# Expert slots dealt in strides, and three kept output tiles, in a float32 block with a 32-expert mixture

## The chip, the cores and the metric

The kernel runs on one core of one Trainium2 chip, as one launch. The metric is the device time of one execution in microseconds (us), as the median of the runs shown.

## What is computed

Two blocks run one after the other on 1024 tokens of 1024 float32 values. The first has a gated linear attention, a pooled branch and, at its end, a mixture of experts; the second has a short convolution and three dilated window attentions. The change is in the mixture of experts of the first block. Cut to what matters, it is

```
g_p, g_idx = top_k(softmax(h @ w_rg + b_rg), 1)            # one of 4 groups
e_top, e_idx = top_k(logits of that group's 8 experts, 2)  # two of its 8 experts
gate = g_p * softmax(e_top)
y[assignment] = gate * (silu(x @ w_gate[e]) * (x @ w_up[e])) @ w_down[e]
out[token] += y of its two assignments
```

So 1024 tokens make 2048 assignments to 32 experts of width 256. Each expert's three weight matrices are 1 MB each, 3 MB together.

## The kernel before, in words

All products are made in three passes: both factors are split into a rounded high part and a rest (`split`, lines 131 to 137: ScalarE makes the high part, VectorE the rest), and `mm3` (lines 166 to 169) adds three matmuls. So every weight tile that arrives costs ScalarE and VectorE an instruction each before TensorE can use it.

**Places and slots.** The router gives each assignment a place within its expert (`posk`, line 688): 0, 1, 2 and so on. Each expert has `CAP` = 96 slots, one for each partition of a tile of 96 rows. For each token tile, lines 690 to 695 compare a constant row 0, 1, ..., 127 (`iota_s`, lines 399 to 400) with the places and get a 0/1 matrix `sel`; matmuls with it (lines 718 to 724) put, for every expert, the token's number and the assignment's number into the slot that the place names (`row_idx`, `row_place`, lines 739 to 747). A slot that no assignment fills gets a number out of bounds. Assignments from place 96 on would be done by a loop behind the experts (lines 1239 to 1322), whose number of turns is computed on the chip.

**One expert.** `fetch` (line 1095) gathers an expert's rows from memory by an indirect DMA on GpSimd's queue, partition p getting the row that slot p names (lines 1074 to 1077); an out-of-bounds slot moves nothing. `turn_rows` transposes them, `into` makes the gate and up products, `turn_act` transposes the activation, `down` (lines 1140 to 1157) makes the output product, scales the rows on ScalarE into a tile `yt` (lines 1148 to 1150), and `put_expert` scatters those rows to memory by another indirect DMA on GpSimd's queue (lines 1081 to 1091). The last expert's rows are not read back from memory: `place_last` (lines 1165 to 1172) makes 0/1 rows `picks` with which TensorE adds them to the first 512 tokens (lines 1174 to 1184).

**The order of the work.** The loop over the 32 experts is written out in lines 1217 to 1235. In the turn of expert e, the rows of e + 3 are fetched, the weights of e + 5 are loaded, expert e's gate product is made, the rows of e + 1 are turned, then e - 1's activation is turned, e's up product is made, and e - 1's output product. Engines run in order; a scheduler at build time puts each engine's instructions into a sequence, ordered mostly as they are written.

**Buffers.** `load_expert` (lines 272 to 292) makes six loads of 512 KB for an expert, two each of gate, up and down. A load waits for the fifth load before it (`QD` = 5). The loads go round 27 buffers: 4 of tag "wr", 4 of tag "wb" and 19 of tag "blk". The tag "blk" has 26 buffers of 4 KB a partition in all (`NBLK`), which are shared by everything that asks for one with `blk(...)`: during the experts four hold gathered rows (`xg`), and the others go to loads and to the `yt` tiles as they come free. Line 1148 asks for a new `yt` for each expert.

```
        yt = blk("yt", (P, D))
        for n in range(2):
            A.activation(yt[:CAP, halves[n]], yps[n], AF.Copy, scale=row_wgt[:CAP, e:e + 1])
        if e < NE - 1:
            put_expert(e, yt)
```

Of the kernel before, what the change touches and what calls it, by code (L numbers as in the profile page):

```python
# [12 lines left out]
F32 = mybir.dt.float32  # L13
# [4 lines left out]
OP = mybir.AluOpType  # L18
AX = mybir.AxisListType

P = 128
T = 1024
D = 1024
# [4 lines left out]
NE = 32  # L28
NOB = 21
CAP = 96  # L30
# [35 lines left out]
def first_then_second_block(ctx: ExitStack, tc: tile.TileContext, a: dict, out: bass.AP):  # L66
    nc = tc.nc
    V, A, G, PE, SY = nc.vector, nc.scalar, nc.gpsimd, nc.tensor, nc.sync
    late = Later()

    C = ctx.enter_context(tc.tile_pool(name="const", bufs=1))
# [13 lines left out]
    def blk(name, shape=(P, 2, 512), dtype=F32):  # L85
        return B.tile(list(shape), dtype, name=name, tag="blk", bufs=NBLK)

    def psum(shape, name="ps"):
        t = PS.tile([P, 512], F32, name=name, tag="ps")
        n = int(np.prod(shape[1:]))  # L90
        v = t[: shape[0], :n]
        if len(shape) == 3:
            v = v.rearrange("p (a b) -> p a b", a=shape[1])
        elif len(shape) == 4:
            v = v.rearrange("p (a b c) -> p a b c", a=shape[1], b=shape[2])
        return v
# [299 lines left out]
    V.tensor_scalar(tri16[:64, :P], tri16[:64, :P], -1.0 / 16, None, op0=OP.add)  # L396
    V.memset(tri16[:64, P:], 1.0 / 16)
    V.memset(tri16[64:, P:], 0.0)
    iota_s = C.tile([P, P], F32, name="iota_s")
    G.iota(iota_s, pattern=[[1, P]], base=0, channel_multiplier=0, allow_small_or_imprecise_dtypes=True)  # L400
    rank8 = C.tile([P, 8], F32, name="rank8")
    V.tensor_scalar(rank8, iota_s[:, :8], -1.0, 8.0, op0=OP.mult, op1=OP.add)
    pcol = C.tile([P, 1], F32, name="pcol")
    G.iota(pcol, pattern=[[1, 1]], base=0, channel_multiplier=1, allow_small_or_imprecise_dtypes=True)
    cnt = W.tile([P, 4, 16], F32, name="cnt")
    for g, wd in enumerate((2, 4, 8, 16)):
        V.tensor_scalar(cnt[:, g, :], iota_s[:, :16], 1.0, float(wd), op0=OP.add, op1=OP.min)
    V.reciprocal(cnt, cnt)


# [25 lines left out]
    for base in (0, -36):  # L436
        G.affine_select(out=fold, in_=fold, compare_op=OP.not_equal, fill=1.0, base=base, pattern=[[-1, 36]],
                        channel_multiplier=1)
# [63 lines left out]
    at = {}  # L502
# [134 lines left out]
    def small(name, shape, dtype=F32):  # L637
        return R.tile([P] + list(shape), dtype, name=name, tag=name, bufs=1)
# [36 lines left out]
    def places(hf, val, gp, e1, e2):  # L675
        ts = slice(4 * hf, 4 * hf + 4)
        pp = psum((P, 4, NE))
        for i in range(4):
            t = 4 * hf + i
            for tt in range(t):  # L680
                PE.matmul(pp[:, i, :], onesb, asg[:, tt, :], start=tt == 0, stop=False)
            PE.matmul(pp[:, i, :], before, asg[:, t, :], start=t == 0, stop=True)
        ex = small("ex", (4,))
        V.tensor_sub(ex, e2, e1)
        A.activation(ex, ex, AF.Exp)
        pr = small("pr", (4, 2, NE))
        V.tensor_mul(pr, oh[:, ts], pp[:, :, None, :].to_broadcast([P, 4, 2, NE]))
        V.tensor_reduce(posk[:, ts, :], pr, axis=AX.X, op=OP.add)
        sels = []
        for i in range(2):  # L690
            sel = R.tile([P, 4, P], BF16, name="sel", tag="sel", bufs=2)
            pos = posk[:, 4 * hf + 2 * i:4 * hf + 2 * i + 2, :].rearrange("p t k -> p (t k)")
            V.tensor_tensor(sel, iota_s[:, None, :].to_broadcast([P, 4, P]), pos[:, :, None].to_broadcast([P, 4, P]),
                            op=OP.is_equal)
            sels.append(sel)

        def weigh():
            den = small("den", (4,))
            V.tensor_scalar(den, ex, 1.0, None, op0=OP.add)
            V.reciprocal(den, den)  # L700
            w2 = small("w2", (4, 2))
            V.tensor_mul(w2[:, :, 0], gp, den)
            V.tensor_mul(w2[:, :, 1], w2[:, :, 0], ex)
            rest = small("rest", (4, 2))
            V.tensor_copy(wgt[:, 0, ts, :], w2)
            V.tensor_sub(rest, w2, wgt[:, 0, ts, :])
            V.tensor_copy(wgt[:, 1, ts, :], rest)
            V.tensor_sub(wgt[:, 2, ts, :], rest, wgt[:, 1, ts, :])
            V.tensor_mul(val.rearrange("p t k v e -> p (t k) v e")[:, :, 3:, :],
                         oh[:, ts].rearrange("p t k e -> p (t k) e")[:, :, None, :].to_broadcast([P, 8, 3, NE]),  # L710
                         wgt[:, :, ts, :].rearrange("p j t k -> p (t k) j")[:, :, :, None].to_broadcast([P, 8, 3, NE]))

        late.at(1 if hf else PLACES, lambda: slots(hf, val, sels, weigh))

    def slots(hf, val, sels, weigh):
        if hf == 0:
            weigh()
        for v0 in (0, 3):
            ps = psum((P, 3, NE))
            for i in range(4):  # L720
                for k in range(2):
                    PE.matmul(ps.rearrange("p a b -> p (a b)"), sels[i // 2][:, 2 * (i % 2) + k, :],
                              val[:, i, k, v0:v0 + 3].rearrange("p a b -> p (a b)"),
                              start=i == 0 and k == 0, stop=i == 3 and k == 1)
            if hf == 0:
                sums.append(R.tile([P, 3, NE], F32, name=f"sums{v0}"))
                V.tensor_copy(sums[-1], ps)
            else:
                sv = sums[v0 // 3]
                if v0 == 0:  # L730
                    V.tensor_add(sv, sv, ps)
                    sums.append(extra[0].tile([P, NE], I32, name="row_place"))
                    with tc.issue_after(row_places(row_idx, sums[2], sv, NE, R).ins):
                        weigh()
                    continue
                V.tensor_add(sv, sv, ps)
                row_weights(row_wgt, sv[:, 0, :], sv[:, 1, :], sv[:, 2, :])
# [331 lines left out]
    wg, wu, wd = w_experts  # L1069
# [20 lines left out]
            tc.declare_no_dep(ins, other, reason="rows of their own")  # L1090
        puts.append(ins)

    xT, gu, act, aT, yp = {}, {}, {}, {}, {}

    def fetch(e):
        return gather_rows(xg[e % (FA + 1)], row_idx[:, e:e + 1], CAP)
# [13 lines left out]
    def expert_tiles(k, n):  # L1110
        n_split[0] += 1
        if n_split[0] % (3 + NX) < 3:
            return split_tiles(k, n)
        return [E.tile([P, k, n], F32R, name="ehl", tag="ehl", bufs=2 * NX) for _ in range(2)]
# [25 lines left out]
    def down(e):  # L1140
        ah, al = aT[e]
        yps = [psum((CAP, 512)) for _ in range(2)]
        for k in range(2):
            hi, lo = expert_tiles(2, 512)
            split(hi, lo, raws[e][4 + k])
            for n in range(2):
                mm3(yps[n], (ah[:, k, :], al[:, k, :]), (hi[:, n, :], lo[:, n, :]), k == 0, k == 1)
        yt = blk("yt", (P, D))
        for n in range(2):
            A.activation(yt[:CAP, halves[n]], yps[n], AF.Copy, scale=row_wgt[:CAP, e:e + 1])  # L1150
        if e < NE - 1:
            put_expert(e, yt)
        else:
            yhl = [blk("yhl", (P, D), F32R) for _ in range(2)]
            for n in range(2):
                split(yhl[0][:CAP, halves[n]], yhl[1][:CAP, halves[n]], yt[:CAP, halves[n]])
            last_y.extend([yt] + yhl)
# [5 lines left out]
    picks = []  # L1163

    def place_last():
        at = E.tile([P, 5], F32, name="last_at")
        picks.append(blk("picks", (P, 512), F32R))
        V.tensor_copy(last_place, row_place[:, NE - 1:NE])
        V.tensor_copy(at[:, 4:], row_idx[:, NE - 1:NE])
        for i in range(4):  # L1170
            V.tensor_scalar(at[:, i:i + 1], at[:, 4:], float(-P * i), None, op0=OP.add)
            V.tensor_scalar(picks[0][:, i * P:(i + 1) * P], iota_s, at[:, i:i + 1], None, op0=OP.is_equal)

    def add_last(c):
        for y in yc2[c]:
# [13 lines left out]
    load_expert(4, after=fetched[0])  # L1189
    turn_rows(0)  # L1190

    iota_e = iota_s[:, :NE]
    cnt_e = E.tile([P, NE], F32, name="cnt_e")
    more = E.tile([P, NE], F32, name="more")
    scan = [E.tile([P, NE], F32, name=f"scan{i}") for i in range(2)]
# [21 lines left out]
    for e in range(NE):  # L1217
# [14 lines left out]
        if e:  # L1232
            down(e - 1)
    turn_act(NE - 1)
    down(NE - 1)

    xc2, turn_part2 = load_cols(x_acc, "x2c")
    end_reg = nc.values_load(n_more[0:1, 0:1], min_val=0, max_val=NOB)
    with tc.For_i(0, end_reg, 1):
        mine = E.tile([P, NE], F32, name="mine")  # L1240
        left = E.tile([P, NE], F32, name="left")
# [2 lines left out]
        V.tensor_scalar(mine, mine, number, None, op0=OP.is_le)  # L1244
        V.tensor_mul(mine, mine, left)
        part = E.tile([P, 2], F32, name="part")
        V.tensor_mul(left, mine, iota_e)
        V.tensor_reduce(part[:, 0:1], left, axis=AX.X, op=OP.add)
        V.tensor_sub(left, more, ends)
        V.tensor_scalar(left, left, number, None, op0=OP.add)  # L1250
# [7 lines left out]
        pos = E.tile([P, NT, 2], F32, name="pos")  # L1258
# [14 lines left out]
        for t in range(NT):  # L1273
            for k in range(2):
                sel = E.tile([P, P], BF16, name="lsel", tag="lsel", bufs=2)
                V.tensor_scalar(sel, iota_s, pos[:, t, k:k + 1], None, op0=OP.is_equal)
                PE.matmul(sp, sel, rv[:, t, k, :], start=t == 0 and k == 0, stop=t == NT - 1 and k == 1)
        li = E.tile([P, 1], I32, name="li")
        lw = E.tile([P, 1], F32, name="lw")
# [14 lines left out]
        for i, w in enumerate((wg, wu)):  # L1294
            src = w[bass.ds(e_reg, 1)].rearrange("o (p k) n -> p (o k) n", p=P)
            for q in range(2):
                wt = blk("lwt", (P, 4, 256))
                SY.dma_start(wt, src[:, 4 * q:4 * q + 4, :])
                for kk in range(4):
                    k = 4 * q + kk  # L1300
# [23 lines left out]
    for c in range(4):  # L1324
        yc2.append([])
        for k in range(2):
            yt = blk("y2c", (P, 4, 256))
# [586 lines left out]
```

## Time and profile before

| | us |
|---|---|
| median of three runs | 1574.97 (1574.22 to 1577.56) |
| the profiled execution | 1581.15 |
| its span, first to last instruction | 1579.4 |
| TensorE (PE) busy in it | 1513.8 (96%) |
| VectorE (DVE) busy | 1041.1 (66%) |
| ScalarE (ACT) busy | 803.6 (51%) |
| GpSimd (POOL) busy | 153.7 (10%) |

The profile is one execution. Times in it count from its first instruction. In rows of instructions, "out<-in" names the tiles written and read, and what stands in brackets at the end is how long the engine had been idle before, and what ended that. PE is TensorE's matmuls, PEld its weight loads, SPq the queue on which SyncE issues DMAs. The granted clock is 1.00 at 2.4 GHz and 0.50 at 1.2 GHz.

### The profile page before, as it was taken

Reading aid. Unit: us, or ns where it says so; the run is one execution under the profiler, and the core shown is the slowest. Engines: PE = TensorE matmul, PEld = TensorE weight load, DVE = VectorE, ACT = ScalarE, POOL = GpSimd, SP = SyncE. Lnnn points to the kernel's source line nnn. Section 1 sums busy time; section 2 is a strip of 40 time slices with the busy share of each in tenths; the row PEclk is TensorE's granted clock in tenths of the full one; section 3 lists DMA queues with packets and bytes.
Section 4 is the critical chain, followed back from the end, with each engine's and each line's share of the span. In section 5 each row is a group of like instructions: output and inputs, shape, how many; then the busy total and the mean of one; then the engine's idle time right before and its main releaser. Section 6 shows DMA issues by size and latency. Waiting matters only on the chain. (4 is left out here: it accounts for less than half of the span.)

```text
span 1579.4 us, 24063 instructions
## 1 busy us (share of the span) xinstructions
PE 1513.8 (96%) x8694; PEld 1253.4 (79%) x8694; DVE 1041.1 (66%) x2309; ACT 803.6 (51%) x1656; POOL 153.7 (10%) x180
## 2 busy tenths in 40 slices
PE   8999999999999995999989996999999999999999
PEld 6888888887888884998979885788878888777777
DVE  6586444777744346897978887765975645677762
ACT  5534322453433232787879784522543324877750
POOL 2000000000000002231212110200100000022211
PEclk9999999999999997999999997999999999999999
DMA  6223334556422367999999998436534222355545
GB/s 212 81 58 119 95 108 172 185 180 188 120 81 81 120 241 270 301 315 349 340 324 353 308 350 262 146 127 231 186 91 133 92 82 73 95 130 151 143 143 173
DMA packets 175445, 284.59 MB, mean 180 GB/s; under 512 B 33968, under 2 KB 117307, under 8 KB 175196
## 3 DMA queue, kind: packets, MB, share of 16 engines
q1 hardware_dynamic: 161484, 244.19, 47.9%
q0 software_dynamic: 13824, 38.84, 7.3%
q8 instruction: 69, 1.13, 0.3%
q14 instruction: 52, 0.43, 0.1%
q10 hardware_dynamic: 16, 0.00, 0.0%
HBM read 252.30 MB, written 43.78 MB: 187 GB/s over the span
## 5 line engine op out<-in xcount | busy, mean ns | idle before, releaser
L133 ACT CAST wh<-wr 128x512 fp32r<-128x512 f32 (+1 forms) x248 | 170.5, 716 | 344.8 <-PE ps L168 190.5
L133 DVE TENSOR_TENSOR wl<-wr,wh 128x512 fp32r<-128x512 f32 (+1 forms) x248 | 196.0, 808 | 157.0 <-ACT wh L133 149.5
L133 DVE TENSOR_TENSOR wl<-ew,wh 128x1024 fp32r<-128x1024 f32 x144 | 172.5, 1220 | 30.9 <-ACT wh L133 27.6
L167 PE MATMUL ps<-h,wh 128*128 128x512 f32 x448 | 176.0, 393 | 0.0
L169 PE MATMUL ps<-h,wl 128*128 128x512 f32 x448 | 174.6, 390 | 0.0
L168 PE MATMUL ps<-h,wh 128*128 128x512 f32 x448 | 174.5, 390 | 0.0
L133 ACT CAST wh<-ew 128x1024 fp32r<-128x1024 f32 x144 | 149.3, 1049 | 34.2 <-PE ps L169 26.8
L167 PE MATMUL ps<-g,wh 128*128 128x512 f32 x320 | 125.9, 394 | 0.0
L168 PE MATMUL ps<-g,wh 128*128 128x512 f32 x320 | 125.2, 392 | 0.0
L169 PE MATMUL ps<-g,wl 128*128 128x512 f32 x320 | 124.9, 391 | 0.0
L167 PE MATMUL ps<-wh,xh 128*96 128x256 f32 x384 | 109.5, 285 | 0.4 <-ACT act L1128 0.4
L168 PE MATMUL ps<-wl,xh 128*96 128x256 f32 x384 | 108.8, 283 | 0.5 <-DVE wl L133 0.5
L169 PE MATMUL ps<-wh,xh 128*96 128x256 f32 x384 | 108.6, 283 | 0.0
L169 PEld LDWEIGHTS ps<-h,wl 128*128 128x128 f32 x448 | 84.1, 188 | 17.8
L167 PEld LDWEIGHTS ps<-h,wh 128*128 128x128 f32 x448 | 84.1, 188 | 17.6
L168 PEld LDWEIGHTS ps<-h,wh 128*128 128x128 f32 x448 | 84.2, 188 | 17.1
L167 PE MATMUL ps<-wh,g 128*128 128x512 f32 x192 | 76.4, 398 | 0.0
L169 PE MATMUL ps<-wh,g 128*128 128x512 f32 x192 | 75.0, 391 | 0.0
L168 PE MATMUL ps<-wl,g 128*128 128x512 f32 x192 | 74.8, 390 | 0.0
L167 PEld LDWEIGHTS ps<-g,wh 128*128 128x128 f32 x320 | 60.4, 189 | 13.0 <-issue 0.6
L168 PEld LDWEIGHTS ps<-g,wh 128*128 128x128 f32 x320 | 60.4, 189 | 12.5 <-DVE g L136 0.2
L169 PEld LDWEIGHTS ps<-g,wl 128*128 128x128 f32 x320 | 60.4, 189 | 12.5
(467 smaller groups left out, 3520.4 us busy)
## 6 DMA issues: line engine op xcount, KB each, us to landing
wr<-in_w_in_dram SPq DMA_DIRECT2D x128, 512.0 KB
ew<-in_w_exp_down_dram SPq DMA_DIRECT2D x64, 512.0 KB
ew<-in_w_exp_gate_dram SPq DMA_DIRECT2D x64, 512.0 KB
ew<-in_w_exp_up_dram SPq DMA_DIRECT2D x64, 512.0 KB
wr<-in_w_out_dram SPq DMA_DIRECT2D x24, 512.0 KB
xs<-xb_rows POOLq DMA_DIRECT2D x28, 256.0 KB
x<-in_x_dram SPq DMA_DIRECT2D x12, 512.0 KB
zb<-sw_d SPq DMA_DIRECT2D x24, 256.0 KB
```

The lines of the kernel that those rows point to most:

```text
L133: both = A.copy(hi, src), V.tensor_sub(lo, src, hi.bitcast(F32))
L167: PE.matmul(ps, lhs[0], rhs[0], start=start, stop=False)
L168: PE.matmul(ps, lhs[0], rhs[1], start=False, stop=False)
L169: PE.matmul(ps, lhs[1], rhs[0], start=False, stop=stop)
```

## The change

Four things change, all about which slot a place gets, and about `yt`.

A constant `slot_s` takes the place of `iota_s`. Its columns 0 to 95 hold, in column 6a + b, the number a + 16b; columns 96 to 127 hold their own number. Where slots are found (lines 693 and 1276), the places are compared with it, so place a + 16b goes to slot 6a + b. `seq` is the same memory read in the order in which it holds 0, 1, ..., 95; where the plain row was wanted (`rank8`, `cnt`, the overflow loop and `picks`) it is read through `seq`, in steps of six columns, and `picks` is written in two pieces. `yt` is no longer asked for anew: the first three experts make a tile each, and expert e uses the tile e mod 3.

```diff
-    iota_s = C.tile([P, P], F32, name="iota_s")
-    G.iota(iota_s, pattern=[[1, P]], base=0, channel_multiplier=0, allow_small_or_imprecise_dtypes=True)
+    slot_s = C.tile([P, P], F32, name="slot_s")
+    G.iota(slot_s[:, :CAP].rearrange("p (a b) -> p a b", a=16), pattern=[[1, 16], [16, CAP // 16]], base=0, channel_multiplier=0,
+           allow_small_or_imprecise_dtypes=True)
+    G.iota(slot_s[:, CAP:], pattern=[[1, P - CAP]], base=CAP, channel_multiplier=0, allow_small_or_imprecise_dtypes=True)
+    seq = slot_s[:, :CAP].rearrange("p (a b) -> p b a", a=16)
...
-    V.tensor_scalar(rank8, iota_s[:, :8], -1.0, 8.0, op0=OP.mult, op1=OP.add)
+    V.tensor_scalar(rank8, seq[:, 0, :8], -1.0, 8.0, op0=OP.mult, op1=OP.add)
...
-        V.tensor_scalar(cnt[:, g, :], iota_s[:, :16], 1.0, float(wd), op0=OP.add, op1=OP.min)
+        V.tensor_scalar(cnt[:, g, :], seq[:, 0, :], 1.0, float(wd), op0=OP.add, op1=OP.min)
...
-            V.tensor_tensor(sel, iota_s[:, None, :].to_broadcast([P, 4, P]), pos[:, :, None].to_broadcast([P, 4, P]),
+            V.tensor_tensor(sel, slot_s[:, None, :].to_broadcast([P, 4, P]), pos[:, :, None].to_broadcast([P, 4, P]),
...
-    xT, gu, act, aT, yp = {}, {}, {}, {}, {}
+    xT, gu, act, aT, yts = {}, {}, {}, {}, []
...
-        yt = blk("yt", (P, D))
+        if len(yts) < 3:
+            yts.append(blk("yt", (P, D)))
+        yt = yts[e % 3]
...
-            V.tensor_scalar(picks[0][:, i * P:(i + 1) * P], iota_s, at[:, i:i + 1], None, op0=OP.is_equal)
+            row = picks[0][:, i * P:(i + 1) * P]
+            V.tensor_scalar(row[:, :CAP].rearrange("p (b a) -> p b a", a=16), seq, at[:, i:i + 1], None, op0=OP.is_equal)
+            V.tensor_scalar(row[:, CAP:], slot_s[:, CAP:], at[:, i:i + 1], None, op0=OP.is_equal)
...
-        V.tensor_mul(left, mine, iota_e)
+        V.tensor_mul(left.rearrange("p (b a) -> p b a", a=16), mine.rearrange("p (b a) -> p b a", a=16), seq[:, :NE // 16, :])
...
-                V.tensor_scalar(sel, iota_s, pos[:, t, k:k + 1], None, op0=OP.is_equal)
+                V.tensor_scalar(sel, slot_s, pos[:, t, k:k + 1], None, op0=OP.is_equal)
```

## Rows read from the trace of the kernel before

**Rows 1.** The page's slices: busy tenths in 40 equal parts of the span.
```profile
PE   8999999999999995999989996999999999999999
...
DMA  6223334556422367999999998436534222355545
```
**Rows 2.** Windows: us, busy us (instructions) by engine, clock, DMA share, GB/s.
```profile
core 0: us, PE busy (x) PEld busy (x) DVE busy (x) ACT busy (x) POOL busy (x), PEclk, DMA share, GB/s
660.00:940.00 280.00, 267.14 (x1930) 240.96 (x1929) 238.16 (x303) 232.53 (x330) 61.34 (x53) 0.98 0.96 335
...
920.00:940.00 20.00, 19.63 (x144) 17.48 (x144) 18.45 (x27) 18.10 (x27) 2.92 (x3) 1.00 1.01 397
```
**Rows 3.** Timeline of GpSimd: start us, us, instruction; gathers (L1075) and puts (L1082).
```profile
721.93 0.96 POOL L1075 DMA_INDIRECT xg<-h_rows,row_idx  x1 [3.16 <-PE ps L1136]
...
736.97 0.96 POOL L1075 DMA_INDIRECT xg<-h_rows,row_idx  x1 [8.51 <-PE ps L1136]
...
793.98 0.96 POOL L1075 DMA_INDIRECT xg<-h_rows,row_idx  x1 [3.20 <-PE ps L1136]
...
808.73 1.02 POOL L1082 DMA_INDIRECT y_rows<-yt,row_place  x1 [4.30 <-ACT yt L1150]
812.95 0.96 POOL L1075 DMA_INDIRECT xg<-h_rows,row_idx  x1 [3.21 <-PE ps L1136]
...
829.09 0.96 POOL L1075 DMA_INDIRECT xg<-h_rows,row_idx  x1 [8.49 <-PE ps L1136]
```
**Rows 4.** Timeline of ScalarE at three places of the expert stage.
```profile
725.99 1.26 ACT L1150 ACTIVATE yt<-ps,row_wgt 96x512 f32<-96x512 f32 x2 [4.77 <-DMA y_rows<-yt,row_place]
...
818.13 1.26 ACT L1150 ACTIVATE yt<-ps,row_wgt 96x512 f32<-96x512 f32 x2 [5.90 <-DMA y_rows<-yt,row_place]
...
894.82 0.38 ACT L1128 ACTIVATE act<-ps 96x256 f32<-96x256 f32 x1
...
908.53 0.37 ACT L1128 ACTIVATE act<-ps 96x256 f32<-96x256 f32 x1
...
916.08 1.05 ACT L133 CAST wh<-ew 128x1024 fp32r<-128x1024 f32 x1 [3.18 <-DMA ew<-in_w_exp_gate_dram]
...
921.02 0.38 ACT L1128 ACTIVATE act<-ps 96x256 f32<-96x256 f32 x1
```
**Rows 5.** Timeline of TensorE: its three longest idle times within the experts.
```profile
728.26 0.47 PE L167 MATMUL ps<-wh,ah 128*96 128x512 f32 x1 [3.58 <-ACT ah L133]
...
820.40 0.47 PE L167 MATMUL ps<-ehl,ah 128*96 128x512 f32 x1 [4.67 <-ACT ah L133]
...
908.96 0.36 PE L167 MATMUL ps<-ehl,xh 128*96 128x256 f32 x1 [3.60 <-ACT act L1128]
```
**Rows 6.** Window just behind the first of them (columns as in group 2).
```profile
728.80:732.10 3.30, 3.30 (x9) 2.07 (x9) 3.05 (x5) 3.29 (x4) 0.00 (x0) 0.50 1.04 363
```
**Rows 7.** Waits of SyncE's queue, 560 to 980 us: us in total, times, longest.
```profile
SPq L286 <- DMA ew<-in_w_exp_gate_dram: 94.7, 47, 8.6
...
SPq L286 <- DVE wl L133: 6.5, 19, 0.7
```
**Rows 8.** Line 286, 600 to 960 us: issue ns min/median/max, first and last start.
```profile
L286 SPq DMA_DIRECT2D ew<-in_w_exp_down_dram x60: 327/328/1153, 607.8 to 939.2; - x60
```
**Rows 9.** Timeline of SyncE's queue.
```profile
705.92 0.59 SPq L286 DMA_DIRECT2D ew<-in_w_exp_gate_dram  x1
706.56 1.15 SPq L286 DMA_DIRECT2D ew<-in_w_exp_down_dram  x1
715.30 0.93 SPq L286 DMA_DIRECT2D ew<-in_w_exp_gate_dram  x2
...
721.34 2.40 SPq L286 DMA_DIRECT2D ew<-in_w_exp_gate_dram  x2
```
**Rows 10.** Timelines of GpSimd and TensorE at the start of the experts.
```profile
623.28 1.04 POOL L1075 DMA_INDIRECT xg<-h_rows,row_idx  x1 [8.81 <-DVE last_at L1171]
...
631.45 0.88 PE L1104 MATMUL ps<-ident,xg 96*128 96x96 f32 x4 [5.64 <-DMA xg<-h_rows,row_idx]
```
**Rows 11.** Line 1172: ns min/median/max, first and last start.
```profile
L1172 DVE TENSOR_SCALAR picks<-iota_s,last_at x4: 281/281/282, 918.3 to 918.9; 128x128 fp32r<-128x128 f32 x4
```

More of the change, by code (lines that the diff above doesn't have):

```diff
@@ L1190, in first_then_second_block @@
     turn_rows(0)
-    iota_e = iota_s[:, :NE]
     cnt_e = E.tile([P, NE], F32, name="cnt_e")
```

## The prediction

> **What bounds the kernel now.** I read the page's strip of slices first [rows 1]. TensorE is at nine tenths or more in nearly every slice, so the change can only return time where TensorE stands idle. The DMA strip is at nine in the eight slices from 632 to 948 us, which are the experts. There the windows [rows 2] show, from 660 to 940 us, TensorE busy 267.1 of 280 us, DMA engines 96% busy and 335 GB/s moved. So the stage has two near-limits: TensorE's own work, and the stream of expert weights with the row gathers and puts beside it.
>
> The pace of TensorE without a wait is read from the gathers, one per expert [rows 3]: from 793.98 to 812.95 us are two steps, so 9.48 us an expert. The next step in the same rows takes 16.14 us (812.95 to 829.09), and that from 721.93 to 736.97 takes 15.04 us. A third long stretch is in ScalarE's rows [rows 4]: the activations of three experts in a row start at 894.82, 908.53 and 921.02 us, 26.20 us where two steps are 18.96. The three cost 5.56, 6.66 and 7.24 us: **19.5 us** in all. TensorE's idle time in them is 3.58, 4.67 and 3.60 us [rows 5]; most of the rest is the slower clock after each, granted 0.50 in the 3.3 us that the window shows (the 1.2 GHz level) [rows 6].
>
> What ends them differs. In the first two, ScalarE waits 4.77 and 5.90 us at line 1150 to write `yt`, until a put has landed [rows 4]. Before the longer wait, which ends at 818.13, the last put was issued at 808.73 [rows 3], 9.4 us earlier: the new output tile had got the buffer of the expert just before it. ScalarE's next work, the splits that TensorE needs, stands behind that wait. In the third, ScalarE waits for expert weights, 3.18 us at its longest [rows 4].
>
> The weight stream itself is paced by its own landings: SP's queue waits 94.7 us on earlier loads of gate weights alone, against 6.5 us on VectorE's splits freeing a buffer [rows 7]. Loads of down weights, two of an expert's six, are issued 60 times from 607.8 to 939.2 us [rows 8]: 59 steps of 5.62 us, 11.23 us an expert. TensorE eats one in 9.48. The 27 buffers of the ring are a lead of 4.5 experts, 42.7 us of work; at 1.75 us lost per expert it is gone after 24 experts. The third stall comes at expert 27. That fits a stream that is too slow, not an accident.
>
> **The change, part by part.** *Three kept output tiles.* `yt` of expert e now takes the tile of expert e-3, whose put was issued three experts, some 28 us, before; the longest wait seen for a put ended 9.4 us after its issue. Both put stalls go: 5.56 + 6.66 = 12.2 us. But the loads were on their way during those stalls and did not stop, so this alone moves nothing at the end: TensorE would reach the third stall 12.2 us sooner and wait there 12.2 us longer. The gain is real only if the stream gets faster: to have no third stall, its weights (the cast that waits for them starts at 916.08 [rows 4], 308 us after the 607.8 of [rows 8]) must come 19.5 us sooner, which is 6.3%.
>
> *Places in strides.* Slot column c = 6a + b now holds place a + 16b. An expert has 2048/32 = 64 rows on average for its 96 slots; the others hold an index out of bounds and move nothing. If the 96 slots are cut into 16 runs of six, one for each DMA engine, the first engine had 6 + 6 rows of 4 KB per expert from gather and put, the last ones none, and the mean is 4 + 4. A weight load puts 8 rows of 4 KB on each engine, so six loads are 48. The fullest engine goes from 60 rows to 56 per expert, **6.7%** less, and a load lands when its last engine is done. That is an estimate from the code; no row tells which engine moved which slot. It just covers the 6.3%. Bounds: 0, if the rows were spread already, to 6.7%.
>
> *Order of the loads.* The 26 shared buffers less four for gathered rows are 22, for which loads and `yt` compete; a load with no buffer is overtaken by one of another tag. SP's rows show it [rows 9]: a single gate load stands ahead of a down load at 706.56, where in turn it would be two gate, two up, two down, and from that one's end, 707.71, to 715.30 nothing is issued for 7.6 us; a pair in turn, at 721.34, takes 2.4 us. Now 26 - 4 - 3 = 19 are left, exactly the loads' share, so I expect the regular order. Bounds of this: 0 to what the best window shows, 397 GB/s at 920 to 940 us against 335 [rows 2]; at 397 an expert's six loads and 128 rows (3.67 MB) take 9.24 us, under TensorE's 9.48. I take the upper side, since both rates stand in this stage: stream fast enough, third stall gone, **7.2 us**. Next in line is VectorE, with 238 of then some 260 us [rows 2].
>
> *The first gather.* TensorE waits 5.64 us for it; issued at 623.28, it lets TensorE start at 631.45, 8.17 us [rows 10]. Expert rows on the fullest engine fall by a third, so the bounds are 0 and 2.7 us; much of the time is before any data moves, I take **1.0 us**.
>
> *What is added.* `picks`: four compares of 128 columns at 281 ns [rows 11] become four of 96, strided, and four of 32. An instruction of 32 columns takes at most those 281 ns, so this adds up to 1.1 us; were the strided ones twice as long as well, 2.2 us. VectorE is 238 of 280 us busy there [rows 2], and no instruction waits on `picks` before the end of the experts: 0, with 2.2 us if that cover is gone. One more iota on GpSimd at the very start, before any weights have come, costs 0. `sel`, `rank8` and `cnt` keep shape and count. The loop for overflowing experts never ran (its lines have no row), so its lines cost 0.
>
> Sum: 12.2 + 7.2 + 1.0 = 20.4 us. The profiled execution took 1581.15 us (span 1579.4), 6.2 above the median of 1574.97; 1581.15 - 20.4 = 1560.7, and from the median, 1554.5.
>
> **The rivals.** *The stream gains half of what is needed* (3.15% of 308 us, 9.7 us): the third stall stays at 19.5 - 9.7 = 9.8 us. Gain 9.7 + 1 = 10.7: 1564; with less or more, 1562 to 1569. For it: 60 to 56 only just covers the need, and batches may remain.
>
> *The stream stays as it is*, because the slots are not cut in runs of six, so that the strides do nothing: the put stalls turn into one of 19.4 us at the weights. 1575, within 0.2%. Against it: the DMA engines are 96% busy by the mean at a rate a sixth below the best window, as unevenly filled engines would show. That 96 partitions go over 16 engines is also what the Trainium skill says (DMA: Bandwidth & Descriptors, Why a DMA increments its semaphore by 16), which no row here shows.
>
> *Slower: the engine that lands last is one that had no rows.* Then today's 11.23 us per expert is its 48 rows, 234 ns each, and its 56 rows will take 13.1 us. It decides from 10.8 us per expert on (the lead of 42.7 us spread over 32 experts is 1.33 us over the 9.48), so over 193 ns a row. After a lead of 4.5 experts the last weights come 27.5 x 1.87 = 51 us later, about 1626 us. Against it: 397 GB/s in a window with puts in it, in which no engine can be at 234 ns a row (16 rows of 4 KB in 234 ns are 280 GB/s). The same page says (Latency and other measured facts) that DMA engines 7 and 15 are usually slower than the others; engine 15 would be such a one, and by that rule the sum would be this 1626. The window's rate speaks against it, but only as a mean.
>
> **How the numbers follow.** Forecast, 1550.5 to 1562 us: 0.72. Half the stream, 1562 to 1569: 0.16. Unchanged: 0.06. Slower: 0.06. The low end is the best of the bounds, 19.5 + 2.7 = 22.2 us, so 1552.8; the three runs of before lie within 3.3 us, and I go 2.3 us lower for that. I give 1550.5 to 1569. A change under 0.2% (3.1 us) can't be told from none here. Faster by more 0.88, within it 0.06, slower 0.06.
>
> **What would show it.** No wait of line 1150 for a put; no half clock between 660 and 930 us; gathers 9.5 us apart throughout; SP issuing gate, up, down in turn, waiting now on VectorE's splits; experts' last `yt` some 20 us sooner. Wrong if ScalarE still waits for weights late in the stage, or if a new wait of about 20 us stands where the third stall was.

## The result and the profile after

The changed kernel takes 1560.28 us (median of 4 runs, 1558.50 to 1560.78), beside 1575.92 of the kernel before (4 runs, 1574.22 to 1577.56). The ratio is 0.9896, with a 95% interval of 0.988 to 0.9911: 15.6 us faster. The profiled execution took 1560.78 us, its span is 1559.1: 20.4 us under the one shown of before. Why these two gains differ is told below.

The page's slices of the changed kernel, which answer to [rows 1]:
```profile
PE   8999999999999996899999996999999999999998
...
DMA  7223334465342366999999988527424231356445
```
Slices are 39 us long. Those from 663 to 936 us, up to the end of the experts, are all at nine tenths on TensorE; before, the one from 790 us had an eight. The strip of nines of the DMA engines is one slice shorter. The window of the same kernel for [rows 2] (columns as there):
```profile
660.00:940.00 280.00, 278.25 (x2042) 252.56 (x2038) 254.64 (x327) 249.25 (x353) 64.32 (x54) 1.00 0.98 350
```
TensorE is busy 278.3 of 280 us where it was 267.1, and the granted clock is 1.00 in the mean. The DMA engines moved 350 instead of 335 GB/s. GpSimd's timeline, the stretches of [rows 3]:
```profile
721.24 0.99 POOL L1080 DMA_INDIRECT xg<-h_rows,row_idx  x1 [2.01 <-PE ps L1141]
...
730.72 1.08 POOL L1080 DMA_INDIRECT xg<-h_rows,row_idx  x1 [1.90 <-PE ps L1141]
...
806.59 1.09 POOL L1080 DMA_INDIRECT xg<-h_rows,row_idx  x1 [1.91 <-PE ps L1141]
...
816.07 0.98 POOL L1080 DMA_INDIRECT xg<-h_rows,row_idx  x1 [2.02 <-PE ps L1141]
...
825.56 1.09 POOL L1080 DMA_INDIRECT xg<-h_rows,row_idx  x1 [1.91 <-PE ps L1141]
```
The gathers come 9.48 us apart, where steps of 15.04 and 16.14 us stood. What ScalarE still waits for, 640 to 945 us (us in total, times, longest):
```profile
ACT wh L133 <- PE ps L169: 18.9, 56, 0.5
...
ACT wh L133 <- DMA ew<-in_w_exp_gate_dram: 2.4, 1, 2.4
ACT yt L1157 <- PE ps L169: 1.4, 1, 1.4
ACT wh L133 <- DMA ew<-in_w_exp_up_dram: 0.8, 2, 0.5
...
ACT wh L133 <- DMA ew<-in_w_exp_down_dram: 0.7, 1, 0.7
```
No row says that `yt` waited for a put, as in [rows 4]. Of the waits for weights the longest is one of 2.4 us. On TensorE it comes through as this, for [rows 5], its first idle time over 0.1 us from 640 us on (two more, of 0.27 and 1.03 us, follow at 930 and 937 us):
```profile
902.07 0.36 PE L167 MATMUL ps<-wh,xh 128*96 128x256 f32 x1 [0.38 <-ACT act L1133]
```
The loads of down weights, for [rows 8], and the waits of SyncE's queue, 560 to 980 us, for [rows 7]:
```profile
L286 SPq DMA_DIRECT2D ew<-in_w_exp_down_dram x60: 327/328/1119, 607.5 to 917.9; - x60
```
```profile
SPq L286 <- DMA ew<-in_w_exp_gate_dram: 87.9, 52, 6.3
SPq L286 <- DMA ew<-in_w_exp_up_dram: 75.1, 40, 8.9
SPq L286 <- DMA ew<-in_w_exp_down_dram: 68.5, 42, 6.2
...
SPq L286 <- DVE wl L133: 5.6, 18, 0.7
```
59 steps in 310.4 us are 5.26 us each, 10.52 us an expert: 6.3% under 11.23. But SP still waits for landings, hardly for VectorE. The loads don't go in turn either; its timeline, for [rows 9]:
```profile
691.38 0.33 SPq L286 DMA_DIRECT2D ew<-in_w_exp_gate_dram  x1
691.80 12.15 SPq L286 DMA_DIRECT2D ew<-in_w_exp_up_dram  x4
704.04 0.38 SPq L286 DMA_DIRECT2D ew<-in_w_exp_gate_dram  x1
```
Four up loads stand between two gate loads. The first gather on GpSimd, and TensorE behind it, for [rows 10]:
```profile
623.02 1.05 POOL L1080 DMA_INDIRECT xg<-h_rows,row_idx  x1 [8.80 <-DVE last_at L1178]
```
```profile
630.60 1.52 PE L1109 MATMUL ps<-ident,xg 96*128 96x96 f32 x8 [5.04 <-DMA xg<-h_rows,row_idx]
```
7.58 us instead of 8.17. And `picks`, for [rows 11] (ns min/median/max):
```profile
L1180 DVE TENSOR_SCALAR picks<-slot_s,last_at x4: 300/306/311, 900.2 to 901.3; 128x96 fp32r<-128x96 f32 x4
L1181 DVE TENSOR_SCALAR picks<-slot_s,last_at x4: 232/236/294, 900.4 to 901.5; 128x32 fp32r<-128x32 f32 x4
```
Four times 306 and 236 ns are 2.2 us for 1.1 before, beside other work.

### The profile page after: what moved, and what is told of

It reads as the page before. It is cut to its first block, busy times and chain, and to the rows that moved or that the text cites. A ratio compares the mean times of both kernels' runs of the same rounds, so it can differ in the third digit from the quotient of the medians.

```text
span 1559.1 us, 24063 instructions
## 1 busy us (share of the span) xinstructions
PE 1506.9 (97%) x8694; PEld 1250.2 (80%) x8694; DVE 1041.8 (67%) x2313; ACT 805.9 (52%) x1656; POOL 157.2 (10%) x181
## 5 line engine op out<-in xcount | busy, mean ns | idle before, releaser
L167 PEld LDWEIGHTS ps<-g,wh 128*128 128x128 f32 x320 | 60.4, 189 | 13.1 <-issue 0.6
L1646 DVE CUSTOM_DVE_ANT_0 sb<-ps,b 128x192 f32<-128x192 f32 (+2 forms) x192 | 56.9, 348 | 20.6 <-PE ps L1640 15.3
```

Of the source, the lines that this page charges most:

```text
L167: PE.matmul(ps, lhs[0], rhs[0], start=start, stop=False)
L1646: s_min = V.tensor_tensor_reduce(out=p, in0=sp[h][:, i, :n], in1=bias, scale=1.0, scalar=3.0e38, op0=OP.add, op1=OP.min, accum_out=stat[:, ...
```

## The experiments

Twelve kernels, in three batches on one chip each, the kernel before among them. The number that they turn on is the time of the weight stream per expert, worked out as above from the row of the down loads.

**Three kept tiles alone** (the kernel before, with only this):
```diff
-        yt = blk("yt", (P, D))
+        if len(yts) < 3:
+            yts.append(blk("yt", (P, D)))
+        yt = yts[e % 3]
```


> The three kept output tiles alone; places lie together as before, and all engines' instructions are in the order of the changed kernel. Theory A (the end of the experts is set by the weight stream, and the strides are what made the stream faster): no wait of yt for a put, but the stream still takes about 11.2 us per expert, a wait for weights late in the experts has grown to 10 to 19 us, and the time is 1571 to 1577 us, within 0.3% of before. Theory B (the kept tiles, by the waits they remove and the order of loads they bring, are the whole gain): stream at 10.5 us per expert, no late wait over 3 us, time 1559 to 1563 us.

Measured: 1576.3 us, ratio 0.9993 (0.9977 to 1.0009). The waits of ScalarE, 640 to 960 us, name DMA in these rows alone:
```profile
ACT wh L133 <- DMA ew<-in_w_exp_gate_dram: 11.2, 5, 5.5
ACT wh L133 <- DMA ew<-in_w_exp_up_dram: 6.8, 7, 3.3
...
ACT ehl L133 <- DMA ew<-in_w_exp_up_dram: 1.9, 2, 1.5
```
The wait for puts is gone; 19.9 us of waiting for weights stand in its place. The waits for puts had given the stream time to catch up; without them the time is spent waiting for weights. Theory A has it so, and theory B falls.

**Strides alone** (the changed kernel, with a new `yt` for each expert, as before):
```diff
-        if len(yts) < 3:
-            yts.append(blk("yt", (P, D)))
-        yt = yts[e % 3]
+        yt = blk("yt", (P, D))
```


> The strides alone; yt is asked for anew for each expert, and SyncE's queue issues the loads in the order of the kernel before. Theory A: the two waits of yt for a put stay where they were (about 5 us each on ScalarE, 12 us of TensorE's time together), the late wait for weights is gone or under 3 us, the stream takes 10.4 to 10.8 us per expert, and the time is 1567 to 1573 us. Theory B: nothing gained, 1574 to 1577 us, with the late wait for weights as before.

Measured: 1567.12 us, ratio 0.9937 (0.9915 to 0.9958). Its down loads, and its waits:
```profile
L286 SPq DMA_DIRECT2D ew<-in_w_exp_down_dram x60: 327/328/1880, 607.0 to 915.9; - x60
```
```profile
ACT yt L1155 <- DMA y_rows<-yt,row_place: 8.1, 3, 3.9
...
ACT wh L133 <- DMA ew<-in_w_exp_down_dram: 0.5, 1, 0.5
```
10.47 us an expert, no late weights, and the put stalls are back, as theory A has it. So the strides bring the stream, and the tiles are worth some 6.5 us once the stream is fast (ratios of 0.9937 and 0.9896), nothing before.

**Another spread** (the changed kernel, slot 12a + b holding place a + 8b):
```diff
-    G.iota(slot_s[:, :CAP].rearrange("p (a b) -> p a b", a=16), pattern=[[1, 16], [16, CAP // 16]], base=0, channel_multiplier=0,
+    G.iota(slot_s[:, :CAP].rearrange("p (a b) -> p a b", a=8), pattern=[[1, 8], [8, CAP // 8]], base=0, channel_multiplier=0,
...
-    seq = slot_s[:, :CAP].rearrange("p (a b) -> p b a", a=16)
+    seq = slot_s[:, :CAP].rearrange("p (a b) -> p b a", a=8)
...
```


> The changed kernel with slot 12a + b holding place a + 8b, so that places are still spread over all partitions, but each run of 12 slots is filled from its front: in runs of six slots, every other run is full (6 rows) and the next has about 2. Every engine's instructions are in the order of the changed kernel. Theory A with runs of six slots per DMA engine: the fullest engine has 60 rows per expert again, so this is as the kept tiles alone, 1571 to 1577 us, stream about 11.2 us per expert. If any spread over the partitions does it (another cut of the slots into engines, or the memory's ports): as the changed kernel, 1559 to 1563 us, stream about 10.5 us.

Measured: 1575.9 us, ratio 0.9992 (0.9977 to 1.0007), 21.9 us of waits for weights, and 11.17 us an expert by the row
```profile
L286 SPq DMA_DIRECT2D ew<-in_w_exp_down_dram x60: 327/328/929, 607.1 to 936.7; - x60
```
Of an average expert's 64 rows, the first eight of every twelve slots are live here. Cut in runs of six, every other run is still full, as before, though the rows lie over all the slots here too. That this gains nothing and the strides of 16 do is what runs of six on one engine each would give.

No row of the profile names the engine of a slot, but the traces list every DMA packet. A gather or a put leaves 4096 bytes for each row, 4 bytes for each empty slot, and 16 more of 4 bytes. So an empty slot does move something, other than the text ahead of the prediction says, but little: its packet takes some 9 ns, that of a row 159 ns or more. Among gathers and puts of 50 to 52 rows, at most 9 rows were in flight at once in the kernels without strides, and up to 16 with strides of 16. Nine is what runs of six give. Runs of eight on twelve engines would give seven, and runs of three and three all sixteen, before as well. Of the 378 gathers and puts that stand apart in the 14 traces, none has more rows in flight than runs of six have engines; both other cuts are exceeded again and again, if an engine moves one row at a time. The same packets show that the experts do not have 64 rows each but 41 to 91. With the rows per expert that the reference's inputs give, the strides leave 9.0 rows on the fullest engine in the mean, in place of 12: with the 48 of weights 57 in place of 60, which is 5% and not the 6.7% of an expert of 64.

**The kernel before once more:**

> The kernel before, once more, for its profile. If the profiled execution shown first was slower than the median because its late wait for weights was longer than usual: here that wait is shorter, and the experts end earlier by the difference, some 3 to 6 us. If the difference to the median lies elsewhere: the three stalls cost 19 to 20 us as before.

Measured: 1576.38 us (one run), span 1574.7, 4.7 us under the execution shown of before. The waits on a put are 8.6 us in two, for 10.7:
```profile
ACT yt L1150 <- DMA y_rows<-yt,row_place: 8.6, 2, 5.1
ACT ehl L133 <- DMA ew<-in_w_exp_up_dram: 4.3, 1, 4.3
ACT wh L133 <- DMA ew<-in_w_exp_gate_dram: 3.1, 1, 3.1
```
Same stalls, other sizes. The experts end 1.7 us sooner than in the one shown (their last `yt`, below), which is less than the 3 to 6 expected of a shorter wait for weights. For this trace the view of DMA issues also gives the median us from issue to landing (last column), 640 to 900 us; first this kernel, then that with the strides alone:
```profile
ew<-in_w_exp_down_dram SPq DMA_DIRECT2D x47, 512.0 KB, 8.4
ew<-in_w_exp_gate_dram SPq DMA_DIRECT2D x47, 512.0 KB, 9.2
ew<-in_w_exp_up_dram SPq DMA_DIRECT2D x46, 512.0 KB, 8.9
```
```profile
ew<-in_w_exp_up_dram SPq DMA_DIRECT2D x50, 512.0 KB, 7.8
ew<-in_w_exp_down_dram SPq DMA_DIRECT2D x50, 512.0 KB, 8.2
ew<-in_w_exp_gate_dram SPq DMA_DIRECT2D x49, 512.0 KB, 7.9
```
A load lands 0.9 us sooner with the strides. A load starts when the one five before it has landed (the window of five loads, lines 286 to 289), so six loads take 6/5 of one load's turn: 11.16 us are turns of 9.30, of which 8.8 from issue to landing; 10.47 are turns of 8.73, of which 8.0. That raised a question: is the limit the engine with most rows, or that window of five loads?

**Places turned by half** (the kernel before; slots 48 to 95 hold places 0 to 47; the other readers of `iota_s` read it in the order of places):
```diff
-    G.iota(iota_s, pattern=[[1, P]], base=0, channel_multiplier=0, allow_small_or_imprecise_dtypes=True)
+    for c0, n, p0 in ((0, 48, 48), (48, 48, 0), (CAP, P - CAP, CAP)):
+        G.iota(iota_s[:, c0:c0 + n], pattern=[[1, n]], base=p0, channel_multiplier=0, allow_small_or_imprecise_dtypes=True)
...
```


> The kernel before, with the places turned by half an expert: slots 48 to 95 hold places 0 to 47, slots 0 to 47 hold places 48 to 95. Theory A (the DMA engine with most rows sets the stream, whichever engine it is; six consecutive slots to one engine): some engine still has 6 + 6 rows per expert, only others than before; down loads of 11.1 to 11.2 us an expert as in the kernel before, time within 0.3% of it, 1572 to 1581 us. Theory E (the engines at the end of the row are slower by themselves and land last, with 48 rows of weights and no expert rows before): they now have 60 rows, 11.2 x 60/48 = 14 us an expert, and the time rises by tens of us, over 1600. If the engines at the start were the slow ones, the time would fall by up to 10 us.

Measured: 1573.85 us, ratio 0.9954 (0.9937 to 0.9971), 11.01 us an expert. Not slower by tens of us, so the engines at the end, which had few rows or none, are not the slow ones: theory E falls. A gain of half a per cent was not expected by theory A either; 11.01 is just under its 11.1. It lies on the side of the third case, slow engines at the start (up to 10 us faster; it is 7.3), which this run does not rule out. If that is the cause, it is a matter of 2%: 184 ns a row for 187. Why the half matters stays open. The kernel before stood higher in this batch (1579.99) than in the others (1575.9 to 1578.8).

**A window of eight loads,** in the kernel before and in the changed one:
```diff
-QD = 5
+QD = 8
```


> The kernel before, in which a weight load waits for the landing of the load eight before it instead of five. Theory A (the fullest DMA engine has work all the time already): down loads stay at 11.0 to 11.2 us an expert, time within 0.3% of before, 1572 to 1581 us, and a load takes longer from issue to landing, some 14 instead of 8.4 to 9.2 us. Theory W (with five loads in flight the engines run dry between a landing and the next issue; evening out the rows only hid that): the stream goes towards the best window's 397 GB/s, under 10 us an expert, the wait for weights goes and the waits on puts stay, so a gain of 7 to 9 us, 1567 to 1570.

> The changed kernel, with the same wider window of eight loads. Theory A: all engines are nearly even already and busy, 10.4 to 10.6 us an expert, a wait for weights of at most 2.5 us stays late in the stage; 1558 to 1562 us, within 0.2% of the changed kernel. Theory W: under 10 us an expert, no wait for weights, 1 to 2 us faster than the changed kernel, 1557 to 1559.

Measured: before 1572.24 us, ratio 0.9946 (0.9929 to 0.9962); changed 1559.68, ratio 0.9865 (0.9847 to 0.9883). The row of the down loads of the first:
```profile
L286 SPq DMA_DIRECT2D ew<-in_w_exp_down_dram x60: 224/328/710, 607.6 to 916.2; - x60
```
10.46 us an expert with the places not dealt at all. It waits for no weights; the waits on puts stay, 7.4 us. Theory A, that the fullest engine has work all the time, falls here; theory W is right on the direction and the gain, not on the rate (under 10). The changed kernel's stream goes to 9.76 us, and SP then waits for VectorE to free buffers, 640 to 900 us:
```profile
SPq L286 <- DVE wl L133: 71.2, 68, 2.6
SPq L286 <- DMA ew<-in_w_exp_gate_dram: 36.1, 15, 4.8
```
So theory W has the rate of the stream right here, but the time is that of the changed kernel: TensorE had nothing left to wait for.

**Two kept tiles** in the changed kernel:
```diff
-        if len(yts) < 3:
+        if len(yts) < 2:
...
-        yt = yts[e % 3]
+        yt = yts[e % 2]
```


> The changed kernel with two kept output tiles instead of three. Theory A: a put lands some 7.2 us after its issue (median) and the tile is wanted again two experts, 19 us, later, so no wait on a put; the 20th buffer goes to the loads and changes little: 1558 to 1562 us, stream 10.4 to 10.6 us an expert. Theory K (three were needed, since now and then a put lands late, or since the regular use of the other 19 buffers matters): waits on puts or on weights of 3 us and more, 1563 or above.

Measured: 1559.57 us, ratio 0.9869 (0.9851 to 0.9886), no wait on a put, 10.22 us an expert. So theory A holds, and two are enough. The stream is 3% faster in this one trace, for no time; that the buffer given back does it is not shown (with the window of eight, below, two tiles gain nothing on the stream).

**Kept tiles and a window of eight, no strides:**

> The kernel before (places not dealt in strides) with the three kept output tiles and the window of eight loads. Theory F (time of the stream per expert is the rows on its fullest DMA engine times a price per row that the window sets: 187 ns with five loads, 174 with eight): 60 rows x 174 ns = 10.4 to 10.5 us an expert, as fast as the strides made it with five; with the tiles kept, no wait on a put and at most 2.5 us of a wait for weights; 1559 to 1564 us, as the changed kernel, without strides. Theory S (only the strides make the put stalls avoidable; without them the stalls turn into waits for weights): 1568 to 1578 us.

Measured: 1568.8 us, ratio 0.9928 (0.9904 to 0.9953), 10.70 us an expert. Theory F falls: the time is over its 1564 us and the waits for weights over its 2.5. Theory S has both right, at the low end of its 1568 to 1578 us. On top of the window the tiles bring at most a few us (0.9946 to 0.9928, intervals that overlap), since 12.0 us of waits for weights come in place of the 7.4 for puts, nearly all in two rows:
```profile
ACT wh L133 <- DMA ew<-in_w_exp_gate_dram: 7.5, 2, 5.3
ACT ehl L133 <- DMA ew<-in_w_exp_up_dram: 3.7, 1, 3.7
```
Why its stream is slower than the 10.46 us of the window alone is open.

**The changed kernel again, the edits for two tiles and the window of eight together, and a window of four:**
```diff
-QD = 5
+QD = 4
```


> The changed kernel once more, beside the others of this batch: 1558 to 1562 us; stream 10.4 to 10.6 us an expert if its one look was typical, 10.2 if the kernel with two kept tiles only fell on a better run.

> The changed kernel with two kept tiles and the window of eight. Theory F: TensorE already has almost no wait in the experts, so nothing is left to gain: 1557 to 1561 us, within 0.15% of the changed kernel of this batch. Theory M (the faster stream also frees something at the start or the end of the experts): 3 us or more faster, below 1557.

> The changed kernel with a window of four loads. Theory F: the price per row rises over 187 ns, 11.0 to 11.8 us an expert, the lead of 42.7 us is used up and the wait for weights is back, 12 to 30 us in all: 1570 to 1590 us. Theory A as it stood (only the fullest engine counts, 56 rows): 10.4 to 10.6 us an expert, 1558 to 1562.

Measured: 1559.78 us, ratio 0.9873 (0.9855 to 0.989), 10.49 us an expert; 1559.15, ratio 0.9865 (0.9848 to 0.9881), 9.81 us an expert; and with four 1574.51, ratio 0.9972 (0.995 to 0.9995), 11.11 us an expert, with 17.8 us of waits for weights. In the last two theory F holds: nothing was left to gain with eight loads, and a window one load narrower takes back what the strides brought, where theory A had 10.4 to 10.6 us an expert. No version is faster than the changed kernel by more than the intervals.

All in one table; "rows" are those on the fullest engine per expert, in the mean (60 or 57 with the 48 of weights, as counted above; theory F was reckoned with 56), and ns per row is the stream's time over them:

| kernel | window | rows | us per expert | ns per row |
|---|---|---|---|---|
| before, shown / again | 5 | 60 | 11.23 / 11.16 | 187 / 186 |
| kept tiles alone | 5 | 60 | 11.11 | 185 |
| spread by 8 | 5 | 60 | 11.17 | 186 |
| turned by half | 5 | 60 | 11.01 | 184 |
| strides alone | 5 | 57 | 10.47 | 184 |
| changed / again | 5 | 57 | 10.52 / 10.49 | 185 / 184 |
| two tiles | 5 | 57 | 10.22 | 179 |
| before | 8 | 60 | 10.46 | 174 |
| kept tiles | 8 | 60 | 10.70 | 178 |
| changed / two tiles | 8 | 57 | 9.76 / 9.81 | 171 / 172 |
| changed | 4 | 57 | 11.11 | 195 |

At a given window the time goes with the rows of the fullest engine, within some 4%, and the window sets the price per row. The runs bear out this product, not either factor alone. At eight with strides the buffers limit too, so those 171 and 172 are upper bounds. Why a wider window lowers the price is not shown. Engines without work explain a part at most: from 660 to 900 us the DMA share is 0.97 in the kernel before and 0.99 with eight loads, while the rate goes from 333 to 353 GB/s.

## Why the prediction was right, and where not

*Faster, within the range:* right, 1560.28 us in 1550.5 to 1569, and the likeliest case.

*Kept tiles, 12.2 us, real only if the stream gets faster:* right in mechanism. Alone they moved nothing (0.9993), and the stall moved on to the weights. That 12.2 was the price in one execution, and the three stalls together cost less in another (below); with the strides in place the tiles measured some 6.5 us.

*Strides, 6.7%, just covering 6.3%:* right in size, 11.23 to 10.52 us, 6.3%, but in part by luck: 6.7% is the gain of an expert of 64 rows, and with the real rows the same reckoning gives 5%, less than the 6.3% needed. The runs of six, an estimate then, are borne out by the packets. The reason was half of it: the text had SP waiting on its own landings, but made the fullest engine the limit. The window of eight got as much with the slots as before (10.46 us).

*Order of the loads:* wrong. The loads still overtake each other with 19 buffers, SP still waits on landings, not on VectorE's splits, and the strides alone, without the 19, had the fast stream too. The third stall, 7.2 us, went by the strides: with them alone no wait for weights over 0.5 us was left.

*First gather, 1.0 us:* 0.6. *`picks`, up to 1.1 us added and hidden:* 1.0 (2.2 for 1.1), hidden.

*Where the rivals decide:* the slower rival put the mark at 10.8 us an expert. That was too generous: at 10.70 (kept tiles, window of eight) 12 us of waits for weights were still there, at 10.5 they are gone but for one of 2.4. The lead of 42.7 us is an average; that a stream in bursts uses it up sooner would fit, but is not shown. This rival's engine at the end of the row did not decide: turned by half, the end got the rows, and the kernel ran at 0.9954. The Trainium skill (DMA: Bandwidth & Descriptors, Latency and other measured facts) calls DMA engines 7 and 15 usually slower than the others. Of the two against the other fourteen no run here says anything: by runs of six and the real rows, engine 7 had 11 expert rows before, and engine 15 has them when turned.

*The number, 1554.5, 5.8 us too low:* the weak step is the last subtraction. The sum of 20.4 came from one execution and was exact against it (1581.15 to 1560.78), but then it was taken off a median of other executions, and the one other execution of before with a trace had less to lose. From the first gather's issue to the last `yt` the traces of before as shown, of before once more and of after (starts on GpSimd and ScalarE) give
```profile
960.46 0.68 ACT L1150 ACTIVATE yt<-ps,row_wgt 96x512 f32<-96x512 f32 x1
```
```profile
623.64 1.04 POOL L1075 DMA_INDIRECT xg<-h_rows,row_idx  x1 [8.81 <-DVE last_at L1171]
```
```profile
958.72 0.68 ACT L1150 ACTIVATE yt<-ps,row_wgt 96x512 f32<-96x512 f32 x1
```
```profile
940.89 0.68 ACT L1157 ACTIVATE yt<-ps,row_wgt 96x512 f32<-96x512 f32 x1
```
337.2 us (with the 623.28 of [rows 10]), 335.1 and 317.9: the stage gave 19.3 us against the one and 17.2 against the other. Behind the stage, to the end of the span, the second execution of before takes 616.0 us, the one shown 618.9 and that of after 618.2. A part of that is in three windows there, of before as shown, of before once more and of after, each behind a wait of TensorE of 1.9 us for `yT`:
```profile
1520.70:1523.90 3.20, 3.20 (x10) 2.42 (x9) 3.20 (x6) 0.76 (x2) 0.00 (x0) 0.50 1.04 223
```
```profile
1517.70:1520.90 3.20, 3.20 (x16) 2.65 (x15) 3.07 (x6) 0.64 (x2) 0.00 (x0) 1.00 1.01 225
```
```profile
1500.10:1503.30 3.20, 3.20 (x9) 2.44 (x9) 3.19 (x6) 0.94 (x2) 0.00 (x0) 0.50 1.04 224
```
In the first and the third, half the clock is granted (the 1.2 GHz level) and TensorE does 9 or 10 matmuls in place of 16, some 1.3 us of work at the second one's 0.2 us each; the rest is not traced. So 15.6 us against the second execution's span are 17.2 from the stage and 0.6 at its start, less 2.2 behind it. That the medians of the result differ by 15.6 us as well is chance. Beside 13 runs of before with a median of 1578.8, the changed kernel's second batch was 19.0 us faster (1559.78), near the sum. Over all 47 runs of before here the median is 1578.4 us, and 20.4 off that would have been 1558.0; so the three runs that the forecast started from, 1574.97, were low ones. Whether that was luck or the chip they ran on, the runs do not tell.

## What to carry to other kernels

A stall that hides behind another is found by adding up the lead: when a stream is slower than its user, freeing the user gains nothing until the stream gains too, and both changes together are then worth more than each alone. A stream with a fixed number of loads in flight moves that many in the time in which one of them lands and the next is issued (five in 9.30 us here), and the fullest engine has its part in that time. So it was worth dealing the slots of a sparse gather over the engines, and the number of loads in flight should be tried at the same time: here it brought the stream as much. Count the real rows, not the average ones. Take the gain off the time of the execution from which it was read, and read a second one before taking it off a median.

## What was not expected of the hardware

The way in which a gather's rows lie in its slots changed the time in which another queue's loads land by a tenth (8.8 to 8.0 us), while the rows moved stayed the same. Three more loads in flight brought 4 to 7% of stream, one less cost 6% (10.5 to 11.1 us). In a window of 240 us, 660 to 900, the changed kernel with eight loads in flight moved this:
```profile
660.00:900.00 240.00, 240.00 (x1775) 218.73 (x1774) 219.53 (x274) 215.42 (x305) 49.80 (x49) 1.00 1.03 379
```
379 GB/s, 13% over the 335 of [rows 2] (to 940 us). And a wait of TensorE of 1.9 us was followed by half the clock for 3.2 us in one execution and not in another of the same kernel.
